# The SSD part's rstd on its four activation rows instead of on eight products

## The chip, the cores and the metric

One core of one Trainium2 chip runs the whole program. The metric is device time in microseconds (us). The engines in the text are TensorE (PE, with its weight loads PEld), VectorE (DVE), ScalarE (ACT), GpSimd (POOL) and SyncE (SP), whose queue issues the DMAs.

## The reference

A model of two layers on 512 tokens of width 1024, all in float32. In each layer a gated feed-forward block, a mixer and a second feed-forward block are added to x, each behind a normalization. The mixer projects the normalized x to the inputs of three parts side by side: SSD (512 channels), S5 (256) and RWKV7 (256). Their outputs are joined, multiplied by `w_out` and added to x. The SSD part ends in a normalization of its own, and this is what the change is about:

```python
    y = y.reshape(bsz, L, M_WIDTH)
    return rmsnorm(y * jax.nn.silu(z), norm_w)      # in ssd_mixer: y * rsqrt(mean(y*y) + eps) * norm_w
...
        y = jnp.concatenate([y_m, y_s, y_r], axis=-1)
        x = x + (y @ w_out[i]).astype(x.dtype)
```

The root, called rstd below, is one number per token. It can be put on the 512 channels of y before the product, or on the result of the product of those channels with `w_out`.

## The kernel before, in words

Activations lie with channels on the 128 partitions and the 512 tokens along the row, so a row of 128 channels is a tile of 128x512, and a weight per channel is a scalar per partition. Every large product is made of float32 operands that are split into a high and a low part (`split`, `split_scaled`, `load_w`): ACT copies the high part (L1428 for the SSD rows, L264 for weights), DVE takes the difference (L1429, L265), and `gemm` (L279, L287, L288) runs three matmuls per 128 input channels. Below, a "part" is these three matmuls.

`mix` works one layer's mixer. Two streams of instructions are written out and then ordered against each other:

- The RWKV part, `rwkv_core` and `rwkv_ends`, runs on small matmuls. The string `ENDS` orders its steps: "Q1" ends with the results for the second half (L1184, L1186), "O0" is the second half of `out(0)`, transposes at L1233 and the scaling L1236, L1238; "o1" is the first half of `out(1)`, L1211 and a normalization over the head (L1217, L1221, L1223, L1225 and small steps); "O1" its second half.
- `stream` is the rest, and `STREAM` orders it. "C" and "Z" are projections for the SSD part, "K" its chunks (`ssd_chunk`; "K13" is group 1, chunk 3, the last), "S" the end of S5. After K13, `ssd_gate` multiplies by silu(z) (L1406), squares (L1407) and adds up two rows (L1409, POOL). "N1" (`ssd_sums`) sums the squares over channels by matmul (L330), takes the root in small steps on DVE and writes two diagonals (L352). "R" (`whole`, `ssd_rstd`) broadcasts the root to all partitions by two matmuls (L361) and a copy on ACT (L364), into the tile `rstd`.
- "T" is a product of the two S5 rows with a column block of `w_out` (two parts, `rows(4, 2)`), "M" one of the four SSD rows (four parts, `rows(0, 4)`); there are eight of each. A product goes into one of three "mm" banks of PSUM. A T result is added to x (L706). An M result is multiplied by `rstd` (L717) and then added (L718); M products that are done before the broadcast wait in `pending`. The SSD rows are split at the first M.
- After the stream come eight products of the two RWKV rows (`rows(6, 2)`), then the next block's normalization.

How the two streams are interleaved on PE is set by cost. Each step yields a cost (0.64 per part of a product, 0.5 for R, 0 for K and N, 3.4 for D), and `quotas` holds the running cost of the RWKV steps with the name of each one's last matmul. The loop at L838 counts the costs of `stream` in `spent`, and two kinds of ordering edges follow:

```python
            while n < len(quotas) - 1 and quotas[n][0] < spent - SLACK:
                n += 1
            self.pin = quotas[n][1] if spent > SLACK else None
...
                if n + LATE < len(heads) and heads[n + LATE] is not None:
                    self.tc.add_manual_dep(heads[n + LATE], name, BEHIND, reason="issue order")
```

The first makes a part of a product follow the RWKV step whose quota it has reached (`SLACK` 7.0). The second makes the first matmul of the step after that (`LATE` 1) follow the last such part. Steps of "K" and "R" have the pin too, N has none. Within these edges a list scheduler places each instruction on its engine. The chunks of "K" use the two "ms" banks of PSUM, four times per chunk. The end of the table of quotas, worked out from the costs in the code, is 67.95 for the last step of Q1, 68.25 for O0, 77.45 for o1 and 77.75 for O1.

Of the kernel before, what the change touches and what calls it, by code (L numbers as in the profile page):

```python
# [13 lines left out]
ADD, SUB, MUL, MAX, MIN = ALU.add, ALU.subtract, ALU.mult, ALU.max, ALU.min  # L14
# [3 lines left out]
L = 512  # L18
D = 1024
# [24 lines left out]
W = 6.0  # L44
RATES = [1.0, 1.0, 1.0, 1.0, 1.0, 1.0, 1.0, 1.0, 1.0, 1.0, 1.0, 0.75, 1.0]
ENDS = "P0 L p1 L p1 L p1 L p1 L p1 L P1 L L q0 L L q0 q0 Q0 L L o0 L q1 q1 L Q1 O0 o1 +8 O1"
STREAM = "D C00 Z00 C02 Z01 C03 c10 C01 k00 C10 k00 c11 k00 K00 k01 k01 C11 k01 K01 K02 K03 N0 C12 C13 K10 Z10 K11 Z11 S K12 T T T K13 N1 T T T T T R M M M M M M M M"
SLACK = 7.0
LAG = 1
LATE = 1  # L50
# [127 lines left out]
class Kernel:  # L178
# [487 lines left out]
    def mix(self, i):  # L666
        nc = self.nc
# [10 lines left out]
        ys = [None] * KD  # L678
        xs = []
# [9 lines left out]
                yield 0.64  # L689
            post(ps)  # L690

        pending = []

        def project(k0, nk, m):
            if k0 == 4 and m % 2 == 0:
                x = self.t(("x", "x", "yf", "b3")[m // 2], [128, 2, L])
                for j in range(2):
                    xs.append(x[:, j])
                    nc.sync.dma_start(out=x[:, j], in_=xd[m + j])
            w = self.load_w(w_out[m, :, k0:k0 + nk], nk, 128)  # L700
            ps = self.bank("mm")
            for q in range(nk):
                self.gemm(ps, w, ys[k0:k0 + nk], [q])
                yield 0.64
            if k0:
                nc.vector.tensor_tensor(out=xs[m], in0=ps, in1=xs[m], op=ADD)  # L706
                return
            pending.append((ps, xs[m]))
            if self.yrs is not None:
                add()  # L710

        def add():

            while pending:
                ps, x = pending.pop(0)
                y = self.t("up", [128, L])
                nc.vector.tensor_tensor(out=y, in0=ps, in1=self.yrs, op=MUL)  # L717
                nc.vector.tensor_tensor(out=x, in0=y, in1=x, op=ADD)  # L718

        def sums(n):  # L720
            self.ssd_sums(n)
# [1 line left out]

        def whole():
            self.ssd_rstd()
            add()
            yield 0.5

        conv = lambda g, j: proj(9 + 6 * g + j, lambda ps: self.ssd_conv(ps, g, j))
# [30 lines left out]

        def rows(k0, nk):
            if k0 == 0 and at[0] == 0:
                ys[0:4] = [self.split_scaled(y, self.p("nw", j)) for j, y in enumerate(self.ym)]
            yield from project(k0, nk, at[k0])
            at[k0] += 1

        def stream():
            self.rwkv_pre()

            together = [first(q) for q in FIRST.split()[:3]]  # L770
            for _ in range(KD + 1):
                for q in together:
                    next(q, None)
            self.seen.update(FIRST.split()[:3])
            for q in FIRST.split()[3:]:
                yield from first(q)
                self.seen.add(q)
            self.seen.add("rwkv")

            runs, done = {}, set()  # L780
            start = {"C": conv, "Z": gate, "K": self.ssd_chunk, "N": sums, "D": steps, "S": s5, "R": whole,
                     "T": lambda: rows(4, 2), "M": lambda: rows(0, 4)}
            for q in STREAM.split():
                n = q.upper()
                if n not in runs:
                    runs[n] = start[n[0]](*map(int, n[1:]))
                if q == n:
                    yield from runs.pop(n)
                else:
                    for _ in range(4 if q[0] in "cz" else 1):  # L790
                        yield next(runs[n])
                    continue
                done.add(q)
                for h in range(2):
                    if len(self.ym) == 2 * h and {f"K{h}3", f"Z{h}0", f"Z{h}1"} <= done:
                        self.ssd_gate(h)
# [55 lines left out]
        for k0, nk in (4, 2), (0, 4), (6, 2):  # L852
            while at[k0] < KD:
                for _ in rows(k0, nk):
                    pass
# [982 lines left out]
```

## Time and profile before

| what | value |
|---|---|
| median of three runs | 2052.49 us (2048.52 to 2055.03) |
| the profiled execution | 2045.95 us, of it 2043.2 us span |
| mean granted TensorE clock | 0.989 of full speed |
| busy share of the span: PE, PEld, DVE, ACT, POOL | 97%, 82%, 75%, 44%, 18% |
| mixer of layer 0, from its first M part to the product behind the broadcast | 653.87 to 668.16 us of the span |

The span goes from the first to the last instruction. A timeline row gives the start, the time taken, the engine, the line of the kernel, the operation with its result and operands, how many such instructions are merged, and in brackets how long the engine stood idle before it and what ended that. The two layers' mixers run the same instructions; the rows below are those of layer 0 where they don't say otherwise.

### The profile page before, as it was taken

To read this page: it belongs to the slowest core of one execution; us is meant where nothing else is said; L and a number is where in the kernel's file an instruction comes from. 1 tells how busy PE (TensorE), PEld (TensorE's weight loads), DVE (VectorE), ACT (ScalarE), POOL (GpSimd) and SP (SyncE) were. 2 spreads that over 40 slices of the span, in tenths; PEclk is the share of its full clock that TensorE was granted. 3 is DMA by queue.
4 is the path that set the end of the run, shared out by engine and by line. 5 is a ranking of instruction groups with operands and counts; after the bars stand their busy time and mean duration, and the time that the engine had idled before them with its cause. 6 is when DMAs were issued, how large, how long until landed. Compare 5 with 4: busy or idle time off the path is not lost.

```text
span 2043.2 us, 39147 instructions
## 1 busy us (share of the span) xinstructions
PE 1979.3 (97%) x15792; PEld 1679.2 (82%) x15792; DVE 1541.7 (75%) x2528; ACT 900.3 (44%) x1374; POOL 363.6 (18%) x715
## 2 busy tenths in 40 slices
PE   8999999998999999999999999999899999999997
PEld 6788888776777789999978999987677678999996
DVE  6646555678568888888887888877956798778886
ACT  4222232443444554444463554454334445444553
POOL 0957667014121000000000000000222200000002
PEclk9999999998999999999999999999999999999998
DMA  4344323431102323333333333354111122333332
GB/s 162 101 129 139 118 85 92 150 98 48 60 22 69 93 88 104 119 109 94 91 116 94 90 108 109 117 197 148 52 47 43 51 88 88 109 100 107 94 109 78
DMA packets 89749, 199.96 MB, mean 98 GB/s; under 512 B 19041, under 2 KB 31329, under 8 KB 89569
## 3 DMA queue, kind: packets, MB, share of 16 engines
q1 hardware_dynamic: 82240, 186.85, 29.4%
q0 software_dynamic: 2592, 9.44, 1.2%
q8 instruction: 124, 2.03, 0.4%
q10 hardware_dynamic: 4736, 1.18, 0.3%
q14 instruction: 57, 0.46, 0.1%
HBM read 184.19 MB, written 12.06 MB: 96 GB/s over the span
## 4 chain that ended last, share of the span: by engine, by line
PE 77%; DVE 11%; issue 4%; DMA 3%; ACT 2%; POOL 1%; SPq 0%; ACTq 0%; POOLq 0%; DVEq 0%
PE mm L279 10%; PE mm L288 9%; PE mm L287 9%; PE mm L453 6%; PE mm L451 6%; PE mm L452 6%; PE ms L288 5%; PE ms L279 5%; PE ms L287 5%; PE mr L452 2%; PE mr L451 2%; PE mr L453 2%; DVE wlo L265 2%; PE ms L298 1%; DMA raw<-in_ffn_wg 1%
## 5 line engine op out<-in xcount | busy, mean ns | idle before, releaser
L264 ACT ACTIVATE whi<-raw 128x512 fp32r<-128x512 f32 (+3 forms) x345 | 250.4, 729 | 479.6 <-PE mm L287 217.3
L279 PE MATMUL mm<-hh,whi 128*128 128x512 f32 x936 | 382.1, 411 | 20.7 <-ACT whi L264 14.6
L288 PE MATMUL mm<-hh,wlo 128*128 128x512 f32 x936 | 370.9, 397 | 0.7 <-DVE wlo L265 0.7
L287 PE MATMUL mm<-hl,whi 128*128 128x512 f32 x936 | 369.7, 395 | 1.4 <-DVE hl L306 1.4
L265 DVE TENSOR_TENSOR wlo<-raw,whi 128x512 fp32r<-128x512 f32 (+3 forms) x345 | 293.8, 854 | 52.2 <-ACT whi L264 51.8
L279 PEld LDWEIGHTS mm<-hh,whi 128*128 128x128 f32 x936 | 178.8, 191 | 67.1 <-ACT whi L264 19.0
L288 PEld LDWEIGHTS mm<-hh,wlo 128*128 128x128 f32 x936 | 177.6, 190 | 41.1 <-DVE wlo L265 1.9
L287 PEld LDWEIGHTS mm<-hl,whi 128*128 128x128 f32 x936 | 178.0, 190 | 35.9 <-DVE hl L306 2.3
L305 ACT ACTIVATE whi<-raw 128x1024 fp32r<-128x1024 f32 x108 | 91.7, 849 | 176.7 <-PE mm L452 85.5
L452 PE MATMUL mm<-b,whi 128*128 128x256 f32 x486 | 134.5, 277 | 0.0
L451 PE MATMUL mm<-b,whi 128*128 128x256 f32 x486 | 134.5, 277 | 0.0
L453 PE MATMUL mm<-b,wlo 128*128 128x256 f32 x486 | 134.5, 277 | 0.0
L453 PE MATMUL mm<-hh,wlo 128*128 128x256 f32 x432 | 121.0, 280 | 1.4 <-DVE wlo L306 1.4
L451 PE MATMUL mm<-hh,whi 128*128 128x256 f32 x432 | 119.3, 278 | 0.0
L452 PE MATMUL mm<-hl,whi 128*128 128x256 f32 x432 | 119.1, 277 | 0.0
L306 DVE TENSOR_TENSOR wlo<-raw,whi 128x1024 fp32r<-128x1024 f32 x108 | 102.6, 950 | 3.3 <-ACT whi L305 2.9
L451 PEld LDWEIGHTS mm<-b,whi 128*128 128x128 f32 x486 | 91.3, 188 | 0.1
L452 PEld LDWEIGHTS mm<-b,whi 128*128 128x128 f32 x486 | 91.3, 188 | 0.1
L453 PEld LDWEIGHTS mm<-b,wlo 128*128 128x128 f32 x486 | 91.3, 188 | 0.0
L453 PEld LDWEIGHTS mm<-hh,wlo 128*128 128x128 f32 x432 | 81.2, 188 | 2.7 <-DVE wlo L306 2.0
L451 PEld LDWEIGHTS mm<-hh,whi 128*128 128x128 f32 x432 | 81.2, 188 | 2.2
L452 PEld LDWEIGHTS mm<-hl,whi 128*128 128x128 f32 x432 | 81.2, 188 | 1.9
(672 smaller groups left out, 5010.6 us busy)
## 6 DMA issues: line engine op xcount, KB each, us to landing
raw<-in_ffn_wu SPq DMA_DIRECT2D x88, 512.0 KB, 3.5
raw<-in_ffn_wg SPq DMA_DIRECT2D x87, 512.0 KB, 3.5
raw<-in_ffn_wd SPq DMA_DIRECT2D x152, 256.0 KB, 2.7
raw<-in_w_in SPq DMA_DIRECT2D x42, 512.0 KB, 3.6
raw<-in_w_out SPq DMA_DIRECT2D x32, 128.0 KB, 2.3
raw<-in_w_out SPq DMA_DIRECT2D x16, 256.0 KB, 2.7
raw<-in_ffn_wd SPq DMA_DIRECT2D x16, 192.0 KB, 2.3
xd<-x SPq DMA_DIRECT2D x12, 256.0 KB, 3.8
```

Of the source, the lines that this page charges most:

```text
L264: nc.scalar.activation(out=hi[:, q], in_=raw[:, q], func=AF.Copy)
L265: sub = nc.vector.tensor_tensor(out=lo[:, q], in0=raw[:, q], in1=hi[:, q].bitcast(F32), op=SUB)
L279: first = nc.tensor.matmul(out=ps, lhsT=hi[:, k], rhs=ah, start=(k == 0), stop=False)
L287: nc.tensor.matmul(out=ps, lhsT=hi[:, k], rhs=al, start=False, stop=False)
L288: mm = nc.tensor.matmul(out=ps, lhsT=lo[:, k], rhs=ah, start=False, stop=(k == last))
L298: mm = nc.tensor.matmul(out=ps, lhsT=a[:, k], rhs=b, start=(k == n == 0), stop=(k == last and n == 2))
L305: self.nc.scalar.activation(out=hi, in_=src, func=AF.Copy)
L306: return self.nc.vector.tensor_tensor(out=lo, in0=src, in1=hi.bitcast(F32), op=SUB)
L451: nc.tensor.matmul(out=ps, lhsT=hi(q), rhs=ah, start=first and q == 0, stop=False, skip_group_check=True)
L452: nc.tensor.matmul(out=ps, lhsT=hi(q), rhs=al, start=False, stop=False, skip_group_check=True)
L453: nc.tensor.matmul(out=ps, lhsT=lo(q), rhs=ah, start=False, stop=last and q == len(ops) - 1, skip_group_check=True)
```

## The change

The four SSD rows are multiplied by `rstd` in place on DVE, ahead of their split at the first M. The results of the M products are then only added to x, as those of T are; `pending` and `add` fall away. In `STREAM`, K13 and N1 stand behind the first T instead of the third, and R behind the second T instead of the eighth. Numbers of the kernel's lines in the text are those of the kernel before.

```diff
--- before.py
+++ after.py
@@ -44,7 +44,7 @@
 W = 6.0
 RATES = [1.0, 1.0, 1.0, 1.0, 1.0, 1.0, 1.0, 1.0, 1.0, 1.0, 1.0, 0.75, 1.0]
 ENDS = "P0 L p1 L p1 L p1 L p1 L p1 L P1 L L q0 L L q0 q0 Q0 L L o0 L q1 q1 L Q1 O0 o1 +8 O1"
-STREAM = "D C00 Z00 C02 Z01 C03 c10 C01 k00 C10 k00 c11 k00 K00 k01 k01 C11 k01 K01 K02 K03 N0 C12 C13 K10 Z10 K11 Z11 S K12 T T T K13 N1 T T T T T R M M M M M M M M"
+STREAM = "D C00 Z00 C02 Z01 C03 c10 C01 k00 C10 k00 c11 k00 K00 k01 k01 C11 k01 K01 K02 K03 N0 C12 C13 K10 Z10 K11 Z11 S K12 T K13 N1 T R T T T T T T M M M M M M M M"
 SLACK = 7.0
 LAG = 1
 LATE = 1
@@ -689,8 +689,6 @@
                 yield 0.64
             post(ps)
 
-        pending = []
-
         def project(k0, nk, m):
             if k0 == 4 and m % 2 == 0:
                 x = self.t(("x", "x", "yf", "b3")[m // 2], [128, 2, L])
@@ -702,20 +700,7 @@
             for q in range(nk):
                 self.gemm(ps, w, ys[k0:k0 + nk], [q])
                 yield 0.64
-            if k0:
-                nc.vector.tensor_tensor(out=xs[m], in0=ps, in1=xs[m], op=ADD)
-                return
-            pending.append((ps, xs[m]))
-            if self.yrs is not None:
-                add()
-
-        def add():
-
-            while pending:
-                ps, x = pending.pop(0)
-                y = self.t("up", [128, L])
-                nc.vector.tensor_tensor(out=y, in0=ps, in1=self.yrs, op=MUL)
-                nc.vector.tensor_tensor(out=x, in0=y, in1=x, op=ADD)
+            nc.vector.tensor_tensor(out=xs[m], in0=ps, in1=xs[m], op=ADD)
 
         def sums(n):
             self.ssd_sums(n)
@@ -723,7 +708,6 @@
 
         def whole():
             self.ssd_rstd()
-            add()
             yield 0.5
 
         conv = lambda g, j: proj(9 + 6 * g + j, lambda ps: self.ssd_conv(ps, g, j))
@@ -760,7 +744,9 @@
 
         def rows(k0, nk):
             if k0 == 0 and at[0] == 0:
-                ys[0:4] = [self.split_scaled(y, self.p("nw", j)) for j, y in enumerate(self.ym)]
+                for j, y in enumerate(self.ym):
+                    nc.vector.tensor_tensor(out=y, in0=y, in1=self.yrs, op=MUL)
+                    ys[j] = self.split_scaled(y, self.p("nw", j))
             yield from project(k0, nk, at[k0])
             at[k0] += 1
```

## Rows read from the trace of the kernel before

**Rows 1.** The page, part 1: busy us (share of the span) and instructions per engine
```profile
PE 1979.3 (97%) x15792; PEld 1679.2 (82%) x15792; DVE 1541.7 (75%) x2528; ACT 900.3 (44%) x1374; POOL 363.6 (18%) x715
```

**Rows 2.** The list of waits, engine PE, whole span: us in total, times, longest us
```profile
PE mm L279 <- DVE up L717: 2.9, 2, 1.5
...
PE mr L1211 <- DVE bon L1236: 2.3, 2, 1.2
```

**Rows 3.** Timeline, engine PE, layer 0: start us, us, what [idle before <-releaser]
```profile
638.98 0.73 PE L1346 MATMUL ms<-b,low 128*128 128x512 f32 x2
...
653.87 0.50 PE L279 MATMUL mm<-hh,whi 128*128 128x512 f32 x1
...
654.66 0.60 PE L1233 MATMUL mr<-cst,kk 128*128 128x128 f32 x4
655.10 0.95 PE L330 MATMUL ms<-cst,kr 128*128 128x1 f32 x8
655.98 0.69 PE L1211 MATMUL mr<-ES,qr 64*32 64x64 f32 x32
657.82 0.69 PE L1211 MATMUL mr<-ES,qr 64*32 64x64 f32 x32 [1.16 <-DVE bon L1236]
658.44 0.50 PE L279 MATMUL mm<-hh,whi 128*128 128x512 f32 x1
...
666.06 0.39 PE L361 MATMUL ms<-tm,ones 128*128 128x512 f32 x1
...
668.16 0.51 PE L279 MATMUL mm<-hh,whi 128*128 128x512 f32 x1 [1.47 <-DVE up L717]
```

**Rows 4.** Timeline, engine DVE, layer 0
```profile
637.59 0.41 DVE L1391 TENSOR_TENSOR b<-ms,b 128x256 f32<-128x256 f32 x1
...
650.18 0.68 DVE L1406 TENSOR_TENSOR b<-b,sg 128x512 f32<-128x512 f32 x1
...
653.26 1.77 DVE L1429 SCALAR_TENSOR_TENSOR hl<-b,par,hh 128x512 fp32r<-128x512 f32 x1
...
655.55 0.73 DVE L1429 SCALAR_TENSOR_TENSOR hl<-b,par,hh 128x512 fp32r<-128x512 f32 x1
...
667.42 1.28 DVE L717 TENSOR_TENSOR up<-mm,rstd 128x512 f32<-128x512 f32 x2
...
682.60 0.69 DVE L717 TENSOR_TENSOR up<-mm,rstd 128x512 f32<-128x512 f32 x1 [1.09 <-PE mm L288]
```

**Rows 5.** Timeline, engine ACT, layer 0
```profile
628.25 1.33 ACT L1428 ACTIVATE hh<-b,par 128x512 fp32r<-128x512 f32 x2
...
666.73 0.60 ACT L364 ACTIVATE rstd<-ms 128x512 f32<-128x512 f32 x1
```

**Rows 6.** Timeline, engine POOL, layer 0
```profile
652.74 1.74 POOL L1409 TENSOR_TENSOR kr<-sg,kr 128x512 f32<-128x512 f32 x1 [20.30 <-ACT kr L1407]
```

**Rows 7.** Stretches: us, busy (instructions) of PE, PEld, DVE, ACT, POOL, PEclk, DMA share, GB/s
```profile
626.00:654.00 28.00, 26.93 (x472) 19.16 (x462) 26.94 (x67) 13.57 (x23) 5.06 (x4) 1.00 0.30 93
654.00:668.00 14.00, 11.53 (x114) 9.36 (x114) 13.34 (x45) 3.62 (x6) 0.48 (x1) 1.00 0.23 74
1642.00:1646.00 4.00, 4.00 (x41) 3.15 (x42) 3.29 (x14) 0.00 (x0) 0.00 (x0) 0.61 0.18 66
```

**Rows 8.** Groups of instructions, 626 to 692 us: busy us, mean ns, idle before
```profile
L1429 DVE SCALAR_TENSOR_TENSOR hl<-b,par,hh 128x512 fp32r<-128x512 f32 x4 | 5.1, 1276 | 0.0
```

**Rows 9.** Groups of instructions, engine DVE, 654 to 668 us
```profile
L265 DVE TENSOR_TENSOR wlo<-raw,whi 128x512 fp32r<-128x512 f32 x4 | 2.7, 686 | 0.5 <-ACT whi L264 0.4
...
L1238 DVE SCALAR_TENSOR_TENSOR bon<-bon,par,g 128x256 f32<-128x256 f32 x2 | 0.9, 466 | 0.0
L1236 DVE SCALAR_TENSOR_TENSOR bon<-mr,par,bon 128x256 f32<-128x256 f32 x2 | 0.9, 467 | 0.0
L1217 DVE TENSOR_TENSOR y<-mr,bh 128x256 f32<-128x256 f32 x2 | 0.8, 407 | 0.0
...
L1221 DVE TENSOR_REDUCE gnm<-y 128x8 f32<-128x512 f32 x1 | 0.7, 687 | 0.0
```

## The prediction

> **What bounds the kernel now.** I read the page's first part, then TensorE's waits, then the timelines of PE, DVE, ACT and POOL around the change, last the table of stretches. PE is busy for 97% of the span, DVE for 75% [rows 1]: a change pays only if it closes a hole in PE's row, and costs only if it opens one. Near the change the list of waits has two holes, once per layer each: 2.9 us in all for the product that waits for the multiplication L717, and 2.3 us for L1211 behind L1236 [rows 2]. The first is the one the change is about. In layer 0 (layer 1 repeats it) the first M product's first part stands at 653.87, three more products' worth of parts follow from 658.44, the broadcast's two matmuls stand at 666.06, and the next product waits until 668.16 because all three "mm" banks hold results that need the broadcast [rows 3]. The broadcast's input is late: the gating L1406 starts at 650.18 and the chain of sum, root and diagonals behind it runs until ACT ends rstd at 666.73 + 0.60 = 667.33, 17.2 us later; L717 starts at 667.42 [rows 4, 5].
>
> So each layer loses 1.47 us there. Behind it PE runs without a hole to the end of the M products, and DVE, which once waits 1.09 us for PE at 682.60 [rows 4], has caught up by then. A time won or lost before 668.16 is therefore won or lost whole.
>
> **The change, part by part.** Removed: eight L717 and eight L718 become eight additions. Two back to back take 1.28 us, the second thus 0.60 [rows 4], so DVE loses 8 x 0.60 = 4.8 us per layer between 667 and 685. They stand beside matmuls; PE waits for DVE there only in the hole of 1.47 us. Worth by themselves: that hole and nothing else.
>
> Added: four multiplications per layer of 128x512 in place, 4 x 0.60 = 2.4 us of DVE by the same row; no row shows them, but L1406 has the same form and takes 0.68 [rows 4]. They come ahead of the split of each row (L1428, L1429), so the M products, which needed no broadcast before, now do. One price is uncertain: both inputs of the new ones lie in SBUF. L1429, with two such inputs, took 1.77 us at 653.26, where POOL's L1409 ran, and 0.73 at 655.55 [rows 4, 6]. POOL is busy for 0.48 of the 14 us from 654 on [rows 7], so I take 0.60; at worst one of the four is lengthened by 1.04 us (2.1 in all), inside the range. The Trainium skill, SBUF - State Buffer, section Who interferes with whom, says this of a Vector instruction with two SBUF inputs against a GpSimd one that reads SBUF; by it the new form could be held where the PSUM form L717 could not. The trace agrees with 1.77 against 0.73.
>
> Moved: K13 and N1 go two T products forward, R six. K13 issues two POOL products, N1 one POOL sum (L1409) ahead of it; POOL had been idle before that for 20.30 us [rows 6]. None of the three issues a DMA, and T and M keep their order among themselves, so SP's queue is as before. N1's matmuls (655.10 to 655.98) and R's two (0.7 us) leave the M stretch and stand earlier: no gain, the work is the same.
>
> Not moved, and this decides: the place of the first M product. Costs counted by the loop at L838 (3.4 of D go uncounted, in L818) are 74.78 at its first part in both versions, since T, N and R all stand ahead of it. Minus SLACK this falls between the last two pins of Q1 and O0, so LATE puts PE's L1233 behind that part, and L1233 frees what L1211 needs. That is just the old order: 653.87, 654.66, 655.98 [rows 3]. In the new kernel this part needs the broadcast. Queued behind it on PE are L1233, half of L1211 and all the other M products; no T product is left to fill in. On ACT the first L1428 waits for the multiplication; behind it stand weight splits (L264) of later products only.
>
> PE arrives there at 653.87 + 0.9 (N1) + 0.7 (R) = 655.4. When is rstd there? Call its end Y; it was 667.33.
> - DVE is full all the way: 26.94 of 28 us and 13.34 of 14 [rows 7]. What stood ahead of Y and falls behind it: four L1429 (5.1 busy [rows 8], 4.8 since each overlaps the next by 0.07), the two output steps of the RWKV part, which now follow the first M part (L1236 0.9, L1238 0.9, L1217 0.8, L1221 0.7, L1223 and L1225 of L1221's size [rows 9]: 4.7, and some 0.4 for the small steps between), and about two weight splits L265 (2.7 for four [rows 9], so 1.2 for two, less the overlap): 11.1 us. If DVE stays full, Y = 656.2.
> - By waits, K12 ends at 637.59 + 0.41 [rows 4]; ahead of it two L1428 (1.33 us of ACT) and two L1429 (5.1 - 1.77 - 0.73 = 2.6 us of DVE) go away [rows 4, 5, 8]. K13 starts at 638.98 [rows 3], behind an L1211 to which it was pinned; that pin falls, but it shares the two "ms" banks with K12, so it follows K12's end. At the least Y moves by those 2.6 us and the 1.0 us from K12's end to K13's start, rounded up to 4 in all: Y = 663.3.
> I take Y = 657.0, near the first, since a full engine is the better witness for a chain that runs on it; both ends stay in the range.
>
> From Y to PE: multiplication 0.68, L1428 0.7 (half of the 1.33 of two [rows 5], and a little), 0.1 of handing on: first matmul at 658.5. Then 0.69 for the part and 0.45 more until its low half is there (L1429's 0.73 less the matmul that runs meanwhile), L1233 0.44, half of L1211 0.69, the old wait of 1.16, its other half 0.62, and the eleven parts from 658.44 to 666.06, 7.62 [rows 3]: 11.67 us, so 670.2 against 668.16. **Sum:** +2.0 us per layer, +4.0 in all. Break-even is Y = 655.0; each microsecond of Y is 2 us of the whole.
>
> One more price: after the 1.16 us hole in layer 1 the granted clock fell to 0.61 for the stretch 1642 to 1646 (TensorE at 1.2 GHz for part of it, 2.4 else) [rows 7], which costs (1 - 0.61) x 4 = 1.6 us; in layer 0 the same hole left it at 1.00. I take no change; in the range layer 0 pays too (+1.6) or neither does (-1.6). The Trainium skill, TensorE: Matmul & The Clock Gate, Part 1, says that the slow clock is the default which activity lifts. By that rule a longer hole makes the drop likelier, and the sum would be +5.6; layer 1 agrees, layer 0 does not.
>
> **The rivals.**
> 1. *The broadcast comes in time* (Y up to 653.9). Then the M products start as PE arrives, and 655.4 + 11.2 = 666.6: -1.5 per layer, -3.0 in all, -4.6 if layer 1 also keeps its clock, -6.9 if the new order covers the wait of L1211 too. For it: R may now stand right behind N1, and K13 has lost its pin. Against it: DVE would need to do 13.4 us less before Y, and only 11.1 can be named.
> 2. *The first M part holds PE*, the case of the other side. K13 can't start before K12 has given back the banks, the chain of small steps from L1406 (17.2 us) stays as long, Y = 663.3: first matmul at 664.8, 676.5 instead of 668.16, +8.3 per layer, +16.6, and +1.6 for the clock: +18. It decides from Y = 658.1 on, where the loss is 3.1 us per layer, 6.2 in all. For it: the small steps of the root are interleaved with an RWKV norm in either place. Against it: DVE would have to stand idle for 663.3 - 656.2 = 7 us.
> 3. *The change does not do what it says:* the scheduler fills the earlier room with other DVE work, or PE's order turns out different, and gain and loss are within 1 us.
>
> **How the numbers follow.** The profiled execution took 2045.95 us (span 2043.2), the three runs have the median 2052.49, 6.54 above it. 2045.95 + 4.0 = 2049.95, and with the same 6.54 the forecast is 2056.5 us. Chances: forecast (Y from 655 to 659, 0 to +8) 0.50; rival 1, 0.22; rival 2, 0.20; rival 3, 0.08. A measurement of this kernel can tell about 0.3% (6.2 us) from no change. Faster by more: 0.07 of rival 1: 0.07. Slower by more: rival 2 and the upper part of the forecast with the clock, 0.20 + 0.11 = 0.31. Within: 0.62. The range goes from -6.9, rival 1's end (2045.6), to +18, rival 2 (2070.5); beyond it lie about half of rival 2 and the tails, 0.2 at most.
>
> **What would show it.** Right: L1233 still directly behind the first M part; a wait of that part for L1428 or L1429 of 2 to 5 us per layer; no wait for an L717; rstd's end at 655 to 659; DVE busy some 5 us less in all. Rival 1: that wait under 0.5 us, the span shorter by 3 to 7 us. Rival 2: a wait of over 7 us and a clock below 1.00 behind it in both layers. The prediction is wrong if PE's order puts other work, such as T products, into the hole, or if the time moves where no M product stands.

## The result, and the profile after

The changed kernel took 2078.41 us in the median of five runs (2075.09 to 2080.76) against 2049.53 for five of the kernel before: 28.9 us more by the medians. The ratio of the runs is 1.0132 with a 95% interval of 1.0113 to 1.0151, by which the loss is some 27 us. The profiled execution took 2080.76 us, its span is 2078.8 and its mean granted clock 0.979. Lines in the rows below are those of the changed kernel: L1414 and L1415 are the old L1428 and L1429, L1392 the old L1406, L1395 the old L1409, L1219 the old L1233, L1197 the old L1211, L1332 the old L1346, L1377 the old L1391; L748 is the new multiplication.

First the page of the changed kernel, part 1, against [rows 1].

```profile
PE 1999.1 (96%) x15792; PEld 1692.8 (81%) x15792; DVE 1542.6 (74%) x2520; ACT 900.8 (43%) x1374; POOL 355.6 (17%) x715
```

The matmuls are the same 15792, yet PE is busy 19.8 us longer: part of the loss is not idle time, but the same instructions going slower. DVE's busy time, which was to fall by some 5 us, has not fallen (1541.7 before). Now PE's list of waits, whole span, against [rows 2].

```profile
PE ms L361 <- DVE tm L352: 7.1, 2, 3.5
...
PE mm L279 <- ACT hh L1414: 5.4, 3, 2.2
...
PE ms L330 <- POOL kr L1395: 4.4, 2, 2.2
...
PE mm L287 <- DVE hl L1415: 1.8, 2, 0.9
```

The wait for L717 is gone, as it should be, and so is the one for the bonus L1236. In their place stands the whole chain that leads to the broadcast, once per layer: N1 waits for its squares, R for its diagonals, the first M part for its high half (the third of the L1414 waits stands elsewhere) and then for its low half. The timeline of PE in layer 0 has them in order, against [rows 3].

```profile
627.48 0.69 PE L1197 MATMUL mr<-ES,qr 64*32 64x64 f32 x32
628.10 0.73 PE L1332 MATMUL ms<-b,low 128*128 128x512 f32 x2
...
641.85 0.62 PE L1332 MATMUL ms<-b,low 128*128 128x512 f32 x2
...
657.58 1.05 PE L330 MATMUL ms<-cst,kr 128*128 128x1 f32 x8 [2.21 <-POOL kr L1395]
662.16 0.77 PE L361 MATMUL ms<-tm,ones 128*128 128x512 f32 x1 [3.53 <-DVE tm L352]
...
665.63 0.79 PE L279 MATMUL mm<-hh,whi 128*128 128x512 f32 x1 [2.17 <-ACT hh L1414]
667.35 0.80 PE L287 MATMUL mm<-hl,whi 128*128 128x512 f32 x1 [0.92 <-DVE hl L1415]
...
668.37 1.05 PE L1219 MATMUL mr<-cst,kk 128*128 128x128 f32 x4
669.35 2.23 PE L1197 MATMUL mr<-ES,qr 64*32 64x64 f32 x64
671.52 0.79 PE L279 MATMUL mm<-hh,whi 128*128 128x512 f32 x1
...
681.44 0.39 PE L279 MATMUL mm<-hh,whi 128*128 128x512 f32 x1
```

Between 655.4 and 671.5 PE has only the matmuls of these rows: the T products are used up, the M parts need the broadcast, and the rest of out is ordered behind the first M part. The four waits add up to 8.83 us, where the kernel before has 1.16 + 1.47 = 2.63. The row of 681.44 is the thirteenth M part; the same part stood at 668.16 [rows 3], so layer 0 is 13.3 us late there. The stages of the next block start 14.5 us late, and layer 1's mixer adds 12.1 us. The two profiled executions differ by 35.6 us in all; the rest of that lies outside the two mixers, and single executions of the kernel before differ by 6.5 us among themselves.

Two things are to be seen ahead of the waits. The first 32 of out(0)'s 64 matmuls (L1197, 627.48) now run ahead of K12's, and the other 32 among them (636.23); all 64 used to follow K12. And K13 starts at 641.85, not earlier than 638.98 [rows 3] but 2.9 us later. DVE and ACT show what that does to the chain, against [rows 4, 5]. DVE first.

```profile
641.05 0.42 DVE L1377 TENSOR_TENSOR b<-ms,b 128x256 f32<-128x256 f32 x1
...
653.84 0.69 DVE L1392 TENSOR_TENSOR b<-b,sg 128x512 f32<-128x512 f32 x1
...
661.33 0.69 DVE L352 TENSOR_TENSOR tm<-cst,rrh 128x512 fp32r<-128x512 f32 x1
...
664.13 2.50 DVE L748 TENSOR_TENSOR b<-b,rstd 128x512 f32<-128x512 f32 x4 [1.51 <-ACT rstd L364]
666.54 2.73 DVE L1415 SCALAR_TENSOR_TENSOR hl<-b,par,hh 128x512 fp32r<-128x512 f32 x4
```

ACT ends the broadcast:

```profile
663.50 0.60 ACT L364 ACTIVATE rstd<-ms 128x512 f32<-128x512 f32 x1 [6.79 <-PE ms L361]
```

K12's last step starts at 641.05, 3.5 us later than before; the gating L1392 starts at 653.84, 3.7 us later than in [rows 4]; from there to the end of rstd at 664.10 it takes 10.3 us instead of 17.2. So the chain did get shorter, but it started later. While the chain runs, DVE is no longer full: it is busy for 7.16 of the 10.10 us up to the end of rstd.

```profile
654.00:664.10 10.10, 3.73 (x49) 2.35 (x37) 7.16 (x21) 2.75 (x5) 1.26 (x1) 0.77 0.21 76
```

Last the granted clock, in the table of stretches of the changed kernel (us, busy time of PE, PEld, DVE, ACT, POOL, then PEclk, DMA share, GB/s), against [rows 7].

```profile
658.00:660.00 2.00, 0.64 (x6) 0.55 (x5) 1.20 (x8) 0.00 (x0) 0.00 (x0) 0.86 0.28 88
660.00:664.00 4.00, 1.30 (x2) 0.58 (x2) 2.38 (x10) 0.50 (x1) 0.00 (x0) 0.50 0.08 28
664.00:668.00 4.00, 1.45 (x3) 0.85 (x4) 3.87 (x7) 2.66 (x5) 0.00 (x0) 0.50 0.00 0
668.00:672.00 4.00, 3.97 (x71) 3.05 (x70) 3.62 (x8) 0.00 (x0) 0.00 (x0) 0.50 0.00 0
672.00:676.00 4.00, 4.00 (x11) 3.03 (x11) 2.90 (x8) 1.25 (x2) 0.00 (x0) 0.50 0.00 0
676.00:678.00 2.00, 2.00 (x9) 1.65 (x8) 1.86 (x8) 0.01 (x1) 0.00 (x0) 0.88 0.00 0
```

TensorE runs at 1.2 GHz from 660 to 676, eight microseconds of it while it is fully busy again. From 664 to 676 it was busy 1.45 + 3.97 + 4.00 = 9.4 us at half speed, which at full speed takes 4.7 us less. That is an estimate of the price, worked out from these rows, and clock_kept below tests it.

### The profile page after: what moved, and what is told of

It is laid out like the page before. It is cut to its first block, busy times and chain, and to the rows that moved or that the text cites. A ratio compares the mean times of both kernels' runs of the same rounds, so it can differ in the third digit from the quotient of the medians.

```text
span 2078.8 us, 39136 instructions
## 1 busy us (share of the span) xinstructions
PE 1999.1 (96%) x15792; PEld 1692.8 (81%) x15792; DVE 1542.6 (74%) x2520; ACT 900.8 (43%) x1374; POOL 355.6 (17%) x715
## 4 chain that ended last, share of the span: by engine, by line
PE 77%; DVE 11%; DMA 4%; issue 3%; ACT 2%; POOL 1%; ACTq 0%; SPq 0%; POOLq 0%; DVEq 0%
PE mm L279 10%; PE mm L287 9%; PE mm L288 9%; PE mm L453 6%; PE mm L451 6%; PE mm L452 6%; PE ms L288 4%; PE ms L279 4%; PE ms L287 4%; PE mr L453 2%; PE mr L452 2%; PE mr L451 2%; DVE wlo L265 2%; PE ms L298 1%; DMA raw<-in_ffn_wg 1%
## 5 line engine op out<-in xcount | busy, mean ns | idle before, releaser
L279 PE MATMUL mm<-hh,whi 128*128 128x512 f32 x936 | 387.1, 415 | 22.9 <-ACT whi L264 14.9
L265 DVE TENSOR_TENSOR wlo<-raw,whi 128x512 fp32r<-128x512 f32 (+3 forms) x345 | 300.5, 874 | 55.8 <-ACT whi L264 55.4
```

Source lines behind the costliest of these rows:

```text
L265: sub = nc.vector.tensor_tensor(out=lo[:, q], in0=raw[:, q], in1=hi[:, q].bitcast(F32), op=SUB)
L279: first = nc.tensor.matmul(out=ps, lhsT=hi[:, k], rhs=ah, start=(k == 0), stop=False)
```

## The experiments

Three causes had to be told apart. The *order theory*: R's cost of 0.5, now counted ahead of the last six T products, shifts some of their pins by a step; one T part that fell on the chain step ahead of o0 no longer does, the second kind of edge that held out(0) back has nothing to hang on, and the scheduler puts out(0)'s first half ahead of K12. The *bank theory*: K13 shares its two "ms" banks with K12, so no place in `STREAM` makes it earlier. The *clock theory*: a good part of the loss is TensorE at half speed behind the waits. All the times in one table; each ratio is against runs of the kernel before taken beside it.

| kernel | median us | before beside it | ratio, 95% interval |
|---|---|---|---|
| changed | 2078.41 | 2049.53 | 1.0132 [1.0113, 1.0151] |
| pins_kept | 2069.95 | 2051.65 | 1.0088 [1.0073, 1.0103] |
| clock_kept | 2071.11 | 2051.65 | 1.0092 [1.0075, 1.0109] |
| stream_only | 2055.95 | 2051.65 | 1.0022 [1.0010, 1.0034] |
| k13_mm | 2061.44 | 2051.65 | 1.0040 [1.0026, 1.0055] |
| k13_free | 2057.08 | 2051.52 | 1.0028 [1.0018, 1.0038] |
| k13_free_pool | 2060.41 | 2051.52 | 1.0037 [1.0023, 1.0052] |
| k13_free_cut | 2056.22 | 2052.94 | 1.0015 [1.0001, 1.0029] |
| m3_ms | 2052.19 | 2051.52 | 1.0004 [0.9991, 1.0017] |
| both_waits | 2052.26 | 2051.52 | 1.0005 [0.9992, 1.0019] |
| before_k13 | 2054.65 | 2052.94 | 1.0008 [0.9996, 1.0021] |
| before_k13_back | 2055.57 | 2052.94 | 1.0020 [1.0007, 1.0032] |

**The pins put back (pins_kept).** The changed kernel, with R's cost counted where it was counted before: a step X, `later`, stands in `STREAM` between the last T and the first M.

```diff
         def whole():
             self.ssd_rstd()
+            yield 0.0
+
+        def later():
             yield 0.5
```

> The kernel after, but R costs 0 and its 0.5 is counted behind the last T, so that T3 to T8 keep the pins they had before (the instructions then stand as the new multiplication with the old STREAM gives them). Order theory (PE waits at the first M part for the broadcast, and the lost pin brought the first half of out(0) 10 us forward, in K12's and K13's way): out(0) stands behind the fourth T part again, K13 ends near 649.5 instead of 653.2, rstd is ready near 660.5 instead of 664.1, the run is 5 to 9 us shorter than after, 19 to 24 us above before. Rival (the shifted pins are the whole loss): within 4 us of before.

0.44% less than the changed kernel, some 9 us, and the intervals [1.0073, 1.0103] and [1.0113, 1.0151] don't touch. In the two traces the mixers hold 2.7 and 2.2 us of that. PE's timeline of layer 0 (here L1200 is out, L1335 the start of K13, L330 N1, L361 R):

```profile
638.42 1.01 PE L1200 MATMUL mr<-ES,qr 64*32 64x64 f32 x64
639.36 0.74 PE L1335 MATMUL ms<-b,low 128*128 128x512 f32 x2
...
654.34 1.05 PE L330 MATMUL ms<-cst,kr 128*128 128x1 f32 x8
659.43 0.77 PE L361 MATMUL ms<-tm,ones 128*128 128x512 f32 x1 [4.04 <-DVE tm L352]
...
662.90 0.79 PE L279 MATMUL mm<-hh,whi 128*128 128x512 f32 x1 [2.17 <-ACT hh L1417]
```

And ACT's broadcast:

```profile
660.77 0.60 ACT L364 ACTIVATE rstd<-ms 128x512 f32<-128x512 f32 x1 [5.76 <-PE ms L361]
```

out(0) is whole again and behind K12, N1's wait is gone, and the first M part comes 2.7 us earlier. The order theory is right. It says more: with the pins kept, the engines' instructions come in the same order whether K13, N1 and R stand early in `STREAM` or where they stood. The move in the string does nothing by itself; its only effect in the change is the shift of the pins. What is left is 18.3 us, which the moved multiplication costs with everything else in its old order.

**The clock kept up (clock_kept).** The changed kernel with 34 matmuls more per layer, whose results nobody reads, in its holes (8 behind the last T part, 14 behind N1, 12 behind R):

```diff
+        def idle(name, count):
+            b = self.bank("mm")
+            for n in range(count):
+                mm = nc.tensor.matmul(out=b, lhsT=self.ones, rhs=ys[4][0], start=(n == 0), stop=(n == count - 1))
+                self.behind(mm, name)
...
+                idle(self.gemmed_t, 8)
+                idle(self.summed, 14)
+                idle(self.spread, 12)
```

> The kernel after with 34 matmuls of 128x512 more per layer (8 ahead of N1's sums, 14 ahead of R, 12 ahead of the first M part) that write a bank nobody reads, so that PE works through its hole. Clock theory: the granted clock stays at 1.00 through the M products, the waits at the first M part stay as long, and the run is 8 to 11 us shorter than after (4 to 5 us per layer). Rival (the slow clock only falls into waiting time): within 2 us of after, or longer if the added matmuls hold up N1 and R.

It does more work on the critical engine and is 0.40% faster than the changed kernel, some 8 us; the intervals [1.0075, 1.0109] and [1.0113, 1.0151] only just miss each other. Its table of stretches:

```profile
660.00:664.00 4.00, 3.82 (x15) 2.56 (x15) 2.61 (x9) 0.60 (x1) 0.00 (x0) 1.00 0.00 2
664.00:668.00 4.00, 3.15 (x31) 2.18 (x31) 4.00 (x8) 2.56 (x4) 0.00 (x0) 1.00 0.00 0
668.00:672.00 4.00, 2.92 (x66) 2.32 (x55) 3.87 (x10) 0.00 (x0) 0.00 (x0) 0.72 0.01 4
672.00:676.00 4.00, 4.00 (x17) 3.21 (x16) 2.51 (x5) 1.15 (x2) 0.00 (x0) 0.85 0.00 0
```

In layer 0 the clock holds to 668 and falls then, behind a wait for the low half (0.85 us) and around one for the bonus (1.08 us) that were not filled; in layer 1 it stays at 1.00 through the M parts. So the direction is shown, but not all of the size: counted from K12's first matmul to the thirteenth M part, the trace is 1.7 us shorter than the changed kernel's in layer 0 and 2.8 in layer 1. That is less than the estimate of 4.7; part of the difference is the wait for the bonus, which comes back with 1.1 us in each layer. The rest of the 8 us was not found in these stretches.

**The string alone (stream_only).** The kernel before with the `STREAM` of the change, the one line of the first hunk of its diff; the multiplication stays on the results.

> The old multiplication of the eight results with the new STREAM. Order theory: M products don't need the broadcast, three of them run ahead of it, so the hole stays at 1 to 4 us per layer: 0 to 6 us above before. Rival (the new STREAM is what costs, by K13 coming later): 20 us or more above before.

4.3 us above the kernel before, a seventh of the whole loss. The shifted pins cost little while the M products need no broadcast.

**Two banks for K13 (k13_mm).** pins_kept, and the last chunk takes every other one of its four banks from "mm":

```diff
-"K": self.ssd_chunk,
+"K": lambda g, c: self.ssd_chunk(g, c, ("mm", "ms", "mm", "ms") if (g, c) == (1, 3) else ("ms",) * 4),
```

> pins_kept with the first and third bank of K13 taken from the three mm banks instead of the two ms banks that it shares with K12. If the ms banks tie K13 to K12's end: K13 ends 8 to 10 us earlier than in pins_kept, R's matmuls stand ahead of Q1's last part, rstd is ready before PE reaches the first M part (655), the hole falls under 1 us and the run is at before or 2 to 4 us below it. Rival (DVE is what sets the chain's end, the banks don't matter): within 3 us of pins_kept.

The place was as the bank theory has it, the time was not. PE in layer 0 (L1418 are the low halves, L751 below the new multiplications):

```profile
642.63 1.05 PE L330 MATMUL ms<-cst,kr 128*128 128x1 f32 x8
...
649.84 0.50 PE L361 MATMUL ms<-tm,ones 128*128 128x512 f32 x1
...
654.42 0.50 PE L279 MATMUL mm<-hh,whi 128*128 128x512 f32 x1 [1.04 <-ACT hh L1417]
657.34 0.79 PE L287 MATMUL mm<-hl,whi 128*128 128x512 f32 x1 [2.41 <-DVE hl L1418]
```

DVE's rows of the same stretch, without a gap between them:

```profile
652.93 2.49 DVE L751 TENSOR_TENSOR b<-b,rstd 128x512 f32<-128x512 f32 x4
655.34 0.68 DVE L703 TENSOR_TENSOR b<-mm,b 128x512 f32<-128x512 f32 x1
655.94 0.68 DVE L265 TENSOR_TENSOR wlo<-raw,whi 128x512 fp32r<-128x512 f32 x1
656.54 2.73 DVE L1418 SCALAR_TENSOR_TENSOR hl<-b,par,hh 128x512 fp32r<-128x512 f32 x4
```

Freed of the banks, N1 and R stand 12 and 10 us further forward than in pins_kept and wait for nothing, and the time falls by 0.48%; the intervals [1.0026, 1.0055] and [1.0073, 1.0103] don't touch. Yet the first M part still waits for 3.45 us, because DVE is busy for 12.80 of the 12.90 us from 640 on and for all of 652.9 to 659.2: now the full engine sets the time, the case that the prediction had taken for the kernel as changed.

**Out let go (k13_free), two products on GpSimd (k13_free_pool), four products cut (k13_free_cut).** k13_free lets the M parts hold back nothing of out, so that out(0)'s last four and half of out(1) can fill the hole. The other two build on it.

```diff
+            self.mrow = k0 == 0
...
-                done[n] = self.gemmed
+                if self.mrow is False:
+                    done[n] = self.gemmed
```

> The run with the last chunk's two 'mm' banks, and besides no M part holds back out's next matmuls: out(0)'s last four stand ahead of the broadcast and the last 32 of out(1) ahead of the first M part, where the matmul engine waited 1.04 and 2.41 us. Theory (the first M part is now held by the vector engine, which is full from 640 us on, so its low halves come at 657.3 to 659 whatever the matmul engine does; the 3.2 us of out(0) and out(1) fill the hole): 2 to 5 us below the run with the two banks alone, that is within 3 us of the kernel before, and the half clock shorter than 8 us. Rival 1 (out(1) then waits for the bonus on the full vector engine, 1 to 2 us, and the low halves come 1.75 us later for it): at the run with the banks alone, within 2 us. Rival 2 (the broadcast's chain held it, not the vector engine): the first M part's wait for the low halves goes altogether and the time falls below the kernel before.

By the ratios 0.12% below k13_mm, some 2.5 us. In layer 0 the hole of 3.45 us is now three small waits, 0.51 for the bonus, 0.57 for the high half, 0.99 for ACT's L1181. But the intervals [1.0018, 1.0038] and [1.0026, 1.0055] overlap, so the size of the gain is open.

```diff
-                    nc.vector.tensor_tensor(out=y, in0=y, in1=self.yrs, op=MUL)
+                    (nc.vector if j < 2 else nc.gpsimd).tensor_tensor(out=y, in0=y, in1=self.yrs, op=MUL)
```

> The run above with two of the four new multiplications on GpSimd instead of the vector engine (2 of 4, some 1.25 us of vector work less, and 1.3 us each on GpSimd). If the vector engine's own work sets when the low halves come (theory): they come about 1.2 us earlier in each layer and the time falls by 1 to 3 us against the run above. If the chain to the broadcast sets it (rival): no change, or 1 to 2 us more, because the two products on GpSimd come later than the vector engine's. If the two engines slow each other (second rival): the vector engine's multiplications and low halves beside them take longer than 0.62 and 0.68 us each.

No gain: 1.0037 [1.0023, 1.0052] against 1.0028 [1.0018, 1.0038]. What both rivals named can be read in layer 0, in DVE's rows of k13_free_pool:

```profile
654.46 1.27 DVE L265 TENSOR_TENSOR wlo<-raw,whi 128x512 fp32r<-128x512 f32 x1
...
656.43 0.96 DVE L753 TENSOR_TENSOR b<-b,rstd 128x512 f32<-128x512 f32 x1
```

And in POOL's row beside them:

```profile
653.89 2.95 POOL L753 TENSOR_TENSOR b<-b,rstd 128x512 f32<-128x512 f32 x2 [9.57 <-ACT rstd L364]
```

While POOL multiplies, DVE's instructions with two SBUF inputs take 1.27 and 0.96 instead of 0.68. The Trainium skill, SBUF - State Buffer, section Who interferes with whom, says that such a pair contends; the trace agrees. Besides, DVE's own first multiplication now starts at 656.43, 2.6 us after rstd is there (2.0 in k13_free), behind four other instructions of which the stretched one is the second.

```diff
-                    nc.vector.tensor_tensor(out=y, in0=y, in1=self.yrs, op=MUL)
+                    nc.vector.tensor_tensor(out=y[:, :64], in0=y[:, :64], in1=self.yrs[:, :64], op=MUL)
```

> The run with the two banks and out freed, with each of the four new multiplications cut to the first 64 of 512 columns: the outputs leave out rstd on the other 448 tokens of the SSD part; every dependency stays. Theory (the vector engine is full from 640 us to the first M part, and the four multiplications of 2.5 us in all are 1.9 us of the delay): the low halves come 1.5 to 2 us earlier in each layer, and 3 to 6 us below that run (waits at half clock count double). Rival (the chain from the row sums over the broadcast to the first multiplication sets it): less than 1 us earlier, and within 1.5 us of that run.

DVE's row of the low halves in k13_free, where the bonus L1228, with which the stretch begins, starts at 653.74:

```profile
658.92 1.41 DVE L1421 SCALAR_TENSOR_TENSOR hl<-b,par,hh 128x512 fp32r<-128x512 f32 x2
```

And in k13_free_cut, where that bonus starts at 652.18:

```profile
655.50 2.74 DVE L1421 SCALAR_TENSOR_TENSOR hl<-b,par,hh 128x512 fp32r<-128x512 f32 x4
```

Counted from the bonus they come after 5.18 and 3.32 us, 1.9 us earlier, as a full DVE would have it. The time falls by 0.13%, 2.7 us, just below what was expected, but the intervals overlap: that DVE's own work sets when the low halves come is shown, its price only bounded, from nothing to some 6 us.

**Can what the kernel before waits for be had in another way?** First, on the kernel before, the fourth M product in an "ms" bank (m3_ms):

```diff
-            ps = self.bank("mm")
+            ps = self.bank("ms" if k0 == 0 and m == 3 else "mm")
```

> The kernel before, with one bank changed: the out projection's fourth product over the SSD tiles takes an 'ms' bank instead of an 'mm' one, so that it no longer waits for the first product's eviction, which in the kernel before waits for the broadcast. Theory 1 (the 1.47 us wait of each layer was all that the late broadcast cost the kernel before, so 3 us were to be had without moving anything): no wait of the product's matmuls for that multiplication is left, the other waits of the matmul engine as before, and 2 to 4 us below the kernel before. Rival (the broadcast holds the evictions, and the wait moves on to the next product that wants a bank, or the broadcast's own two matmuls wait for a bank): a wait of 1 us or more stands a product later, and the time within 1 us of before.

Then, besides, a step X, `back`, in `STREAM` between R and the first M, so that two M parts stand ahead of out(0)'s last four (both_waits):

```diff
+        def back():
+            yield -1.0
```

> The kernel before with the bank of the run above, and a step of cost -1.0 ahead of the M steps, which puts two parts of the out projection ahead of out(0)'s second half and one more ahead of the last 32 matmuls of out(1): the waits that the kernel before has at out(1) (1.16 us in layer 0 for the bonus, about as much in layer 1) are filled with work that is ready. Theory: no wait over 0.5 us is left for the bonus, layer 1's half-clock stretch of the kernel before goes with it, and 4 to 8 us below the kernel before. Rival 1 (the parts that are moved forward only wait themselves, for the low halves on the vector engine, 1 us or more in each layer): 1 to 4 us below, as the bank alone. Rival 2 (out(1)'s chain behind it is what sets the end of the layer, and it now starts later): above the run with the bank alone, by 1 to 4 us.

Neither moves the time (1.0004, 1.0005, both intervals hold 1). PE's timeline of m3_ms shows the rival at work:

```profile
671.39 0.40 PE L361 MATMUL ms<-tm,ones 128*128 128x512 f32 x1
671.62 0.39 PE L279 MATMUL ms<-hh,whi 128*128 128x512 f32 x1
...
674.36 0.39 PE L361 MATMUL ms<-sg,ones 128*128 128x512 f32 x1
...
677.12 0.50 PE L279 MATMUL mm<-hh,whi 128*128 128x512 f32 x1 [1.93 <-DVE up L717]
```

The fourth product, with a bank of its own (ms), now stands on PE between the broadcast's two matmuls. One right behind the other in the kernel before (666.06 and 666.29), they are 3.0 us apart; counted from the first M part rstd ends 4.4 us later, and the wait for L717 stands one product further on with 1.93. In both_waits the wait for the bonus falls from 2.3 us in both layers together to 0.5, but the one for L717 grows from 2.9 to 4.5.

Then K13's two "mm" banks on the kernel before (before_k13), and with the M parts drawn forward as above (before_k13_back):

> The kernel before with one edit: the last chunk takes its banks from ('mm', 'ms', 'mm', 'ms'), as in the run with the two banks. rstd stays on the eight results and no multiplication is added. Theory (the two 'ms' banks tied the last chunk to the one ahead of it; freed of them, the row sums and the broadcast come 8 us or so earlier, and a broadcast that comes earlier is worth what the kernel before waited for it): the broadcast's two matmuls stand some 3 products further forward with nothing else changed, no wait for the results' multiplication is left (1.47 us in each layer), and 2 to 4 us below the kernel before. Rival (the 'mm' banks that the last chunk takes are then missing to out(1) and the in projection beside it): a wait of 1 us or more at the last products of out(1)'s tokens, and at the kernel before or above it by up to 3 us.

> The run above and a step of cost -1.0 ahead of the M steps, so that two parts of the out projection over the SSD tiles stand ahead of out(0)'s last four matmuls and one more ahead of the last 32 of out(1). Theory: the wait for the bonus (1.16 us in each layer) is filled as well, no half clock is left in either layer's stretch, and 4 to 8 us below the kernel before. Rival (what out(1) hands on to the group norm now starts later, and the vector engine is what the layer's end waits for): no further gain on the run above, within 1.5 us of it.

K13's end comes 2.2 us earlier, but the broadcast does not. DVE's rows of before_k13, the gating and the second diagonal:

```profile
647.55 0.69 DVE L1406 TENSOR_TENSOR b<-b,sg 128x512 f32<-128x512 f32 x1
...
662.34 0.69 DVE L352 TENSOR_TENSOR sg<-cst,rrmry 128x512 fp32r<-128x512 f32 x1
```

R's first matmul on PE and ACT's broadcast in before_k13:

```profile
666.37 0.40 PE L361 MATMUL ms<-tm,ones 128*128 128x512 f32 x1
...
667.26 0.60 ACT L364 ACTIVATE rstd<-ms 128x512 f32<-128x512 f32 x1 [0.70 <-PE ms L361]
```

The gating starts 2.6 us earlier than in [rows 4], and rstd ends at 667.86 against 667.33: the chain is 20.3 us long instead of 17.2. DVE keeps the head start: the second diagonal is done at 663.03 instead of 665.63. It is lost on PE, where R's matmuls stand behind M parts until 666.37. PE reaches them no earlier, for it now waits 1.23 and 0.61 us for DVE at out, and its clock falls to 0.70 from 660 to 664. The wait for L717 is gone in layer 0 and stays in layer 1 with 1.5. Drawing the M parts forward gives no gain either: 1.0020 is above the kernel before, and overlaps with before_k13. No version that was tried beats the kernel before.

## Why the prediction was wrong, point by point

**Right:** the place of the first M part with out(0)'s last four directly behind it (665.63, 668.37), the wait for L717 gone, and the step from the broadcast to PE: 1.5 us were forecast from rstd's end to the first matmul, 664.10 to 665.63 were measured. That the order of T and M among themselves stays was right too.

**The step that failed is Y.** The prediction put the end of rstd at 657.0; it is 664.10. It chose between a bound by a full DVE (656.2) and a bound by waits (663.3), and took the first, "since a full engine is the better witness for a chain that runs on it". But DVE was full because PE kept feeding it. Once the T products are used up and every M product waits for the chain itself, DVE has little but the chain: it was busy for 7.16 of the 10.10 us up to 664.10, where the kernel before has 12.74 of the 13.40 from 654 to 667.4. The chain did shrink to 10.3 us; the few small steps and the two matmuls run one after the other, and that, not DVE's load, is its length. In pins_kept, where out stands in its old place, rstd ends at 661.37: of the 7.1 us by which Y was off, some 4.4 come from taking the full engine as the bound, and 2.7 from the changed order of out.

**What the bound by waits missed.** It put K12's end earlier and K13 behind it. The tie to K12 was right, as k13_mm shows by undoing it. But K12's end came 3.5 us later, since out(0) now ran ahead of it. And the splits that went away from ahead of K12 bought nothing: even in pins_kept K13 starts at 639.36, against 638.98 before. The order is a step of the prediction, too: costs were compared "in both versions" only at the first M part, where they are equal, and the T parts between R's new place and its old one, which all count 0.5 more, were left out. pins_kept prices it at some 9 of the 27 us.

**N1 and R** were counted as 0.9 and 0.7 us of work that moves ahead of the first M part. They brought their waits with them, 2.21 and 3.53 us, in which PE stands as still as at the M part; both are on the way to Y and count in it.

**The clock** was priced at 0 for the forecast, and at 1.6 us for layer 0 in the range. Half speed lasted 16 us in layer 0, and clock_kept puts its price at some 8 us by the runs, 4.5 by the two traces' M parts. The Trainium skill, TensorE: Matmul & The Clock Gate, Part 1, says that the slow clock is the default which activity lifts; the prediction read from it that a longer hole makes the drop likelier. The trace agrees: here both layers fall to 0.50 (layer 1 from 1668 to 1683).

With four terms the prediction's own sum closes for layer 0. Its break-even is Y = 655.0, so 664.1 costs 9.1; half speed 4.7 by the estimate above; the wait for the low half 0.92 where 0.45 was counted, 0.5 more; and the old wait of 1.16 for the bonus, which was kept in the sum, does not occur: 9.1 + 4.7 + 0.5 - 1.2 = 13.1, against the 13.3 measured at the thirteenth part. The next 1.2 us, up to the 14.5 at the next block, were not followed.

**The rivals.** Rival 2 named the mechanism: K13 cannot start before K12 gives back its banks, and PE stands at the first M part. That its Y = 663.3 lies 0.8 us from the measured 664.10 is luck in part: it had the gating start at some 646.2 and the chain take 17.2 us, and they were 653.84 and 10.3, two errors of some 7 us that cancel. Its price of 18 us fell short of the 27 mainly by the clock, which it put at 1.6. The argument against it, that DVE would have to stand idle for 7 us, was the wrong one to trust. Rival 1 is excluded by the four waits. Rival 3 was half right, in that PE's order did turn out different, but it priced that at nothing.

## What to carry to other kernels

Before moving a factor from a result to an operand, ask what independent work is left to cover its chain: here some 14 us of M products and of out lay over the end of it (653.87 to 668.16), and after the change nothing. An engine that is full says how long its work takes only as long as something feeds it; where the change takes the feeder away, go by the chain of waits. Where an order is made from running costs, a step that is moved changes the count of everything between its old and its new place, so compare the order there too, and not only at the ends.

## What was not expected of the hardware

The half clock outlives its cause. In the changed kernel PE was busy for 3.97 of 4 us from 668 to 672 and for all of 672 to 676, with the granted clock still at 0.50 in both; it came back at 676 to 678 (0.88). By the estimate above the 8.8 us of waits in a layer so cost 4.7 us more, of which clock_kept shows 2.8 in layer 1. Putting 34 idle matmuls into the holes of each layer made the kernel faster, by about 8 us as the runs have it.
